# Finishing the first up tiles from SBUF and moving adaLN loads out of the w_o stage

## The chip, the core and the metric

The kernel runs on one NeuronCore of a Trainium2 chip. A core has five engines with an instruction stream each: TensorE (PE, with its weight loads shown apart as PEld) multiplies matrices into PSUM, VectorE (DVE) and ScalarE (ACT) do elementwise work, GpSimd (POOL) and SyncE (SP) are used here mostly to issue DMAs. An engine works through its stream in order and waits at an instruction until its operands are there. Work passes between engines through SBUF tiles and PSUM banks.

The metric is device time in microseconds for one execution of the whole program, as a median of several runs. A profile is one execution, recorded by the hardware.

## What is computed

One layer of a decoder trunk, for 512 tokens of width 2048, all in float32: a token-mixing part (stick-breaking attention, sparse attention with an index, two gates, an output projection `w_o`) and a gated MLP with a causal convolution of width 3. Both are modulated by a conditioning vector c (adaLN). Cut to what matters here:

```python
c_act = jax.nn.silu(c)
mod = c_act @ w_ada[layer] + b_ada[layer]
sh1, sc1, gt1, sh2, sc2, gt2 = jnp.split(mod[:, None, :], N_MOD, axis=-1)
h = rmsnorm(x, g_mix[layer]) * (1 + sc1) + sh1
x = x + (1 + gt1) * mixer(h, positions, w_in[layer], w_a[layer], w_b[layer], w_o[layer])
h = rmsnorm(x, g_ffn[layer]) * (1 + sc2) + sh2
x = x + (1 + gt2) * conv_ffn(h, w_up[layer], conv_w[layer], conv_b[layer], w_down[layer])
...
def conv_ffn(h, w_up, conv_w, conv_b, w_down):
    u = h @ w_up
    up = jnp.pad(u, ((0, 0), (CONV_WIDTH - 1, 0), (0, 0)))
    u = conv_b + sum(conv_w[i] * up[:, i:i + S] for i in range(CONV_WIDTH))
    a, b = jnp.split(u, 2, axis=-1)
    return (jax.nn.silu(a) * b) @ w_down
```

## The kernel before

**Arithmetic.** Every float32 operand is split into a high part and a rest (wh and wl for weights, lines 168 and 170; pairs of F tiles for activations, lines 197 and 199), and a product is three matmuls (lines 178 to 180). A weight chunk is loaded into one of eight buffers with the tag raw (128x1024, 512 KB), split by ScalarE (wh) and VectorE (wl) into one of three rooms, and then multiplied.

**Units.** Most projections run in `unit` (line 242), which computes two output tiles with seven half-width products of eight pairs each, 168 matmuls of 128x256, in place of eight products. A unit loads four weight quarters into raw, a fifth raw tile s takes their sums and differences (lines 268, 272, 306, 310), and the results are put together from three PSUM banks (lines 276, 308, 309, 312, 314). Units take their banks from acc and att in turn. `between` is called at two places of a unit with the last instructions there, so that other work can be queued behind them.

**Stages, in order.** Values and index queries; 31 units over `w_x` (u = 1 to 31, line 748); the second values projection, in whose sixteen steps the index scores are computed (line 877); eight stick-breaking heads; eight sparse heads (line 1057), with the projection by `w_a` between them; sixteen tiles by `w_b`, merged with the gates (lines 1092 and 1093); eight units over `w_o` (line 1177), the last of which carries the second norm along; the first six tiles of the up projection, done in the plain way (`plain`, line 1226) while the operands of the units are being made; 41 units over `w_up` (line 1357), each followed by `finish`; the down projection.

**adaLN.** mod is made on VectorE: `w_ada` is stored transposed, in tiles of 128 rows and two halves of 1024. A half is loaded into raw and multiplied by the broadcast c in one operation with a running sum (line 711, 1.22 us). 96 halves of tiles 32 to 79 are spread over the stages: `ada_load(n)` loads the next n and `some_ada(n)` takes n products, loading first if nothing is loaded. From the 49th half on, a second broadcast, cb[1], holds one of the eight raw buffers. Seven halves go through a tile of their own (soft, line 735). Tiles 32 to 47 are needed at the end of the sparse heads, 48 to 79 before the last w_o unit. In the kernel before, the w_x units take one each, five stick heads three each, the sparse heads 26 in all, w_b six, and the eleven that remain fall to the w_o units, where `between` calls `some_ada()` and `ada_load()` twice in a unit.

**The plain up tiles.** The first NU = 3 column tiles of each half of w_up are computed plainly in six PSUM banks. They are evacuated into six F tiles, saved to DRAM (ud, line 1295) and brought back one by one in the later up units by `finish_first`, a generator of which one step runs ahead of each unit from j = 9 on; it loads a tile (SP, line 1337), convolves it (ScalarE line 1330, VectorE line 1333), and saves the product (line 1353). `finish` does the same for the units' own tiles, from the F tiles that they return: `conv` (lines 1210 to 1212) into a tile w, of which there are two, a Silu (line 1217), a product (line 1219) and a save to yd by POOL.

**Slots.** F tiles (512 columns) come from a pool of 62. In the up stage 56 hold the operand forms of the units.

**Order.** The building framework orders each engine's instructions, allocates the tiles and sets the waits, by the order of the program and its own estimate of when an operand is ready. An instruction can be put ahead of the place where it stands in the program; `behind(ins)` holds what is traced inside it behind ins on ins's engine.

## Time and profile before

| | us |
|---|---|
| median of 3 runs | 2738.51 (2733.37 to 2740.41) |
| the profiled execution | 2737.63 |
| its span | 2735.7 |
| TensorE busy in the span | 2677.8 |
| VectorE busy | 2406.6 |
| ScalarE busy | 1448.4 |
| w_x units, first to last | 228 to 827 |
| index scores and second values | 827 to 901 |
| sparse heads | about 1010 to 1138 |
| w_b | 1139 to 1226 |
| w_o | 1226 to 1402 |
| plain up tiles | 1402 to 1475 |
| up units | from 1475 |

A row of the page's groups or of the timeline names a line of the kernel, an engine, an operation, the tiles out<-in with buffer numbers left out, their shapes and a count, then busy time and the mean of one in ns, and in the end how long the engine stood idle before it and what ended that. A row of the list of waits names who waited, at which line, for whom, with the total, the number of times and the longest. A row of the table by stretches has a stretch of time, its length, the busy time and the count of instructions of PE, PEld, DVE, ACT and POOL, the granted TensorE clock, the share of time in which the DMA engines were busy, and their GB/s. Matmuls are pipelined and their ends are modelled, so a matmul's duration is longer than the distance to the next; distances between starts are used for TensorE.

### The profile page before, as it was taken

To read this page: it belongs to the slowest core of one execution; us is meant where nothing else is said; L and a number is where in the kernel's file an instruction comes from. 1 tells how busy PE (TensorE), PEld (TensorE's weight loads), DVE (VectorE), ACT (ScalarE), POOL (GpSimd) and SP (SyncE) were. 2 spreads that over 40 slices of the span, in tenths; PEclk is the share of its full clock that TensorE was granted. 3 is DMA by queue.
4 is the path that set the end of the run, shared out by engine and by line. 5 is a ranking of instruction groups with operands and counts; after the bars stand their busy time and mean duration, and the time that the engine had idled before them with its cause. 6 is when DMAs were issued, how large, how long until landed. Compare 5 with 4: busy or idle time off the path is not lost.

```text
span 2735.7 us, 47661 instructions
## 1 busy us (share of the span) xinstructions
PE 2677.8 (98%) x18700; PEld 2453.8 (90%) x18700; DVE 2406.6 (88%) x3402; ACT 1448.4 (53%) x2037; POOL 315.8 (12%) x514
## 2 busy tenths in 40 slices
PE   8999999999999999999999999999999999999998
PEld 6789999999997778889999999999999998887876
DVE  8888989999987899798878999999999997888887
ACT  4444455554446665434466555555555455546443
POOL 0000010100012211112220000000000000003011
PEclk9999999999999999999999999999999999999999
DMA  9883556666676648766864666666666436468785
GB/s 351 326 301 123 174 199 196 192 212 220 205 227 203 199 140 285 237 206 216 243 215 136 189 175 189 173 181 175 171 177 181 132 125 223 154 179 236 207 228 166
DMA packets 167853, 551.65 MB, mean 202 GB/s; under 512 B 21750, under 2 KB 22390, under 8 KB 167628
## 3 DMA queue, kind: packets, MB, share of 16 engines
q1 hardware_dynamic: 119820, 408.49, 46.4%
q0 software_dynamic: 47216, 139.73, 18.7%
q8 instruction: 147, 2.41, 0.3%
q14 instruction: 78, 0.64, 0.1%
q10 hardware_dynamic: 592, 0.39, 0.1%
HBM read 453.97 MB, written 91.14 MB: 199 GB/s over the span
## 4 chain that ended last, share of the span: by engine, by line
PE 83%; DVE 8%; DMA 4%; issue 3%; ACT 2%; SPq 0%; POOL 0%; ACTq 0%; DVEq 0%; POOLq 0%
PE att L180 13%; PE att L179 13%; PE att L178 13%; PE acc L179 12%; PE acc L180 12%; PE acc L178 12%; DVE wl L170 2%; PE acc L928 1%; DMA F<-ud 1%; ACT wh L168 1%; DMA raw<-in_w_down 1%; PE outs L179 1%; PE outs L178 1%; PE outs L180 1%; PE acc L896 1%
## 5 line engine op out<-in xcount | busy, mean ns | idle before, releaser
L168 ACT ACTIVATE wh<-raw 128x1024 fp32r<-128x1024 f32 (+1 forms) x790 | 828.8, 1055 | 945.7 <-DVE raw L272 174.9
L170 DVE TENSOR_TENSOR wl<-raw,wh 128x1024 fp32r<-128x1024 f32 (+1 forms) x790 | 953.4, 1214 | 125.3 <-ACT wh L168 117.7
L178 PE MATMUL acc<-F,wh 128*128 128x256 f32 (+1 forms) x2448 | 702.3, 287 | 9.0 <-DVE sp L308 4.3
L178 PE MATMUL att<-F,wh 128*128 128x256 f32 (+1 forms) x2448 | 704.3, 288 | 6.2 <-DVE sp L308 5.2
L180 PE MATMUL acc<-F,wl 128*128 128x256 f32 (+1 forms) x2448 | 701.5, 287 | 8.1 <-DVE wl L170 8.1
L180 PE MATMUL att<-F,wl 128*128 128x256 f32 (+1 forms) x2448 | 702.3, 287 | 4.3 <-DVE wl L170 4.3
L179 PE MATMUL att<-F,wh 128*128 128x256 f32 (+1 forms) x2448 | 701.6, 287 | 0.2 <-DVE F L199 0.2
L179 PE MATMUL acc<-F,wh 128*128 128x256 f32 (+1 forms) x2448 | 701.2, 287 | 0.1
L178 PEld LDWEIGHTS acc<-F,wh 128*128 128x128 f32 x2448 | 460.2, 188 | 21.8 <-issue 5.1
L178 PEld LDWEIGHTS att<-F,wh 128*128 128x128 f32 x2448 | 461.6, 189 | 17.4 <-issue 5.7
L180 PEld LDWEIGHTS acc<-F,wl 128*128 128x128 f32 x2448 | 460.4, 188 | 18.1 <-DVE wl L170 9.3
L180 PEld LDWEIGHTS att<-F,wl 128*128 128x128 f32 x2448 | 461.7, 189 | 13.2 <-DVE wl L170 5.0
L179 PEld LDWEIGHTS att<-F,wh 128*128 128x128 f32 x2448 | 461.7, 189 | 8.8 <-DVE F L199 0.7
L179 PEld LDWEIGHTS acc<-F,wh 128*128 128x128 f32 x2448 | 460.5, 188 | 10.1 <-DVE F L490 0.8
L178 PE MATMUL att<-wh,F 128*128 128x512 f32 x448 | 177.8, 398 | 0.2 <-ACT wh L168 0.2
L179 PE MATMUL att<-wl,F 128*128 128x512 f32 x448 | 175.3, 391 | 0.7 <-DVE wl L170 0.7
L180 PE MATMUL att<-wh,F 128*128 128x512 f32 x448 | 175.1, 391 | 0.0
L179 PE MATMUL acc<-wl,F 128*128 128x512 f32 x288 | 113.5, 394 | 4.3 <-DVE wl L170 4.3
L268 DVE TENSOR_TENSOR raw<-raw,raw 128x1024 f32<-128x1024 f32 x80 | 97.4, 1218 | 18.9 <-DMA raw<-in_w_o 14.1
L178 PE MATMUL acc<-wh,F 128*128 128x512 f32 x288 | 112.4, 393 | 0.1
L180 PE MATMUL acc<-wh,F 128*128 128x512 f32 x288 | 111.3, 391 | 0.0
L711 DVE SCALAR_TENSOR_TENSOR raw<-raw,raw 128x1024 f32<-128x1024 f32 x89 | 107.3, 1217 | 0.8 <-DMA raw<-in_w_ada 0.8
(370 smaller groups left out, 3719.9 us busy)
## 6 DMA issues: line engine op xcount, KB each, us to landing
raw<-in_w_up SPq DMA_DIRECT2D x164, 512.0 KB, 3.8
raw<-in_w_ada SPq DMA_DIRECT2D x152, 512.0 KB, 5.2
raw<-in_w_x SPq DMA_DIRECT2D x128, 512.0 KB, 4.3
raw<-in_w_down SPq DMA_DIRECT2D x104, 512.0 KB, 4.5
xd<-F POOLq DMA_DIRECT2D x64, 256.0 KB, 3.0
F<-xd POOLq DMA_DIRECT2D x64, 256.0 KB, 4.9
raw<-in_w_o SPq DMA_DIRECT2D x32, 512.0 KB, 5.5
soft<-in_w_gate SPq DMA_DIRECT2D x32, 512.0 KB, 3.9
```

The lines of the kernel that those rows point to most:

```text
L168: pins["wh"] = act(wh, raw, AF.Copy)
L170: pins["wl"] = tt(wl, raw, wh.bitcast(F32), ALU.subtract)
L178: mm(ps, ah, bh, start=first, stop=False, skip_group_check=not check)
L179: mm(ps, ah, bl, start=False, stop=False, skip_group_check=not check)
L180: return mm(ps, al, bh, start=False, stop=last, skip_group_check=not check)
L268: last_v = tt(s, a21, a22, ALU.add)
L711: stt(w, w, 1.0, cb[half], ALU.mult, ALU.mult, accum_out=macc[:, t, half : half + 1])
L896: mm(zk, k[:, q0 : q0 + P], q[:, q0:], start=kb != 3, stop=False, skip_group_check=True)
L928: mm(o, negtri if tri else negones, i, start=False, stop=True, skip_group_check=True)
```

## The change

Plain up tiles: they are evacuated into slots and stay there. The save to ud and `finish_first` are gone, and `finish` runs on each pair of them ahead of the first, second and third up unit.

adaLN halves: three more are loaded and taken in the w_x units 29 and 30, two in the steps of the index scores (loaded at steps 3 and 9, taken at 6 and 12), and three more in each of the last two sparse heads, together eleven. In w_o `between` loads only at its first call and takes only at its second.

```diff
@@ for u in range(1, 32)
         def between(i, *pins):
+            free = u in (29, 30)
             if not i:
+                ada_load(2 if free else 1)
+            elif u == 29:
                 ada_load()
             with behind(*pins):
                 next(work)
-                if i:
-                    some_ada()
+                if i or u == 30:
+                    some_ada(2 if free and i else 1)
@@ index scores
     for i in range(16):
+        if i in (3, 9):
+            ada_load()
         run(fill, 2)
         run(index)
+        if i in (6, 12):
+            some_ada()
     run(fill)
@@ sparse heads
         last = sparse_2(p, s)
         run(fill)
+        if hd > 5:
+            ada_load(3)
         before = hd, sparse_3(p), vb[hd // 4]
         with behind(last):
-            some_ada(2 if hd else 0)
+            some_ada((2 if hd else 0) + (3 if hd > 5 else 0))
         run(fill, 2)
@@ w_o
     def between(i, *pins):
         turn()
         with behind(*pins):
-            some_ada()
-        ada_load()
+            if i:
+                some_ada()
+        if not i:
+            ada_load()
@@ up
             form(f[p], x1[2 * p], x1[2 * p + 1])
-    ud = dram("ud", 2 * NU)
-    for i, ps in enumerate(ups):
-        save(ud[i], evac(ps))
+    ups = [evac(ps) for ps in ups]
...
-    def finish_first():
...
-        for j in range(NU):
-            u = bring(2 * j)
-            yield
-            yield
-            for a in half(2 * j, u):
-                yield
-            act(a, a, AF.Silu)
-            u = bring(2 * j + 1)
-            yield
-            yield
-            for b in half(2 * j + 1, u):
-                yield
-            tt(a, a, b, ALU.mult)
-            save(yd[j // 2][:, j % 2 * S : (j % 2 + 1) * S], a)
-            yield
-
-    gate, first_tiles = last_gate(), finish_first()
+    gate = last_gate()
     for j in range(NU, NJ):
-        if 2 * NU <= j < 2 * NU + 2:
+        if j < 2 * NU:
+            finish(j - NU, *ups[2 * (j - NU) : 2 * (j - NU) + 2])
+        elif j < 2 * NU + 2:
             x = t2k("T", 2)
             save(x, x1d[KT - 2 + j - 2 * NU])
             to_turn.append((KT - 2 + j - 2 * NU, x))
-        if j >= 3 * NU:
-            run(first_tiles)
         finish(j, *unit(A["w_up"][j - NU], f, beside_up))
```

## The prediction

> **What bounds the kernel now.** I read the page first: its span and the busy times.

> ```profile
> span 2735.7 us, 47661 instructions
> PE 2677.8 (98%) x18700; PEld 2453.8 (90%) x18700; DVE 2406.6 (88%) x3402; ACT 1448.4 (53%) x2037; POOL 315.8 (12%) x514
> ```

> TensorE sets the time, with VectorE close behind. A change that touches no matmul can only win what TensorE loses in waits, so I looked for those. I took the start of the first matmul of every seven-product unit from the timeline and asked for the busy times between these starts. First the up stage (columns: stretch, length, then busy time and count of PE, PEld, DVE, ACT, POOL, granted clock, DMA share, GB/s):

> ```profile
> 1475.02:1493.97 18.95, 18.95 (x169) 18.95 (x168) 13.23 (x15) 10.68 (x14) 2.18 (x4) 1.00 0.65 209
> 1493.97:1513.01 19.04, 19.04 (x170) 19.04 (x169) 17.85 (x22) 12.27 (x15) 1.08 (x2) 1.00 0.53 174
> 1513.01:1532.06 19.05, 19.05 (x171) 19.05 (x170) 17.85 (x22) 10.99 (x14) 1.43 (x2) 1.00 0.61 165
> 1532.06:1551.58 19.52, 19.52 (x175) 19.52 (x174) 17.86 (x22) 11.59 (x15) 2.15 (x3) 1.00 0.71 194
> ```

> An undisturbed unit takes 19.04 us, its 168 matmuls end to end. The fourth has four transposes more (19.52). Of the later units eight are longer; they are the ones in which the plain up tiles come back from DRAM. Four of them, and the sum of all eight:

> ```profile
> ...
> 1764.55:1788.10 23.55, 21.17 (x170) 20.78 (x169) 19.21 (x24) 12.20 (x16) 1.42 (x2) 0.93 0.62 162
> 1845.22:1869.29 24.07, 21.26 (x171) 20.86 (x169) 19.69 (x25) 11.68 (x15) 1.98 (x3) 0.93 0.61 160
> 1945.45:1968.28 22.83, 20.98 (x170) 20.79 (x169) 19.21 (x24) 12.21 (x16) 1.42 (x2) 0.93 0.63 168
> 2025.40:2047.35 21.95, 19.62 (x171) 19.22 (x169) 19.07 (x25) 11.68 (x15) 1.98 (x3) 1.00 0.61 156
> ...
> sum 171.89, PE 160.40 PEld 158.24 DVE 151.44 ACT 93.77 POOL 13.04; mean PE 20.05 PEld 19.78 DVE 18.93 ACT 11.72 POOL 1.63
> ```

> Eight undisturbed units would be 8 x 19.04 = 152.32 us, so **19.6 us** are lost here. Next the stage that multiplies by w_o: its first five units, their sum, and the two that follow:

> ```profile
> 1226.17:1249.89 23.72, 20.07 (x170) 19.49 (x168) 23.12 (x34) 10.52 (x15) 1.07 (x2) 1.00 0.44 147
> 1249.89:1272.45 22.56, 20.25 (x178) 20.08 (x177) 18.36 (x24) 10.41 (x15) 4.55 (x7) 1.00 0.73 236
> ...
> 1293.84:1318.13 24.29, 21.44 (x178) 21.27 (x177) 19.48 (x24) 10.95 (x15) 6.46 (x10) 0.95 0.75 226
> ...
> sum 112.77, PE 102.75 PEld 101.51 DVE 96.58 ACT 51.92 POOL 22.04; mean PE 20.55 PEld 20.30 DVE 19.32 ACT 10.38 POOL 4.41
> ```

> ```profile
> 1338.94:1358.94 20.00, 20.00 (x178) 20.00 (x177) 17.48 (x20) 11.02 (x15) 6.36 (x10) 1.00 0.83 251
> 1358.94:1378.94 20.00, 20.00 (x178) 20.00 (x177) 16.39 (x19) 10.39 (x14) 5.45 (x9) 1.00 0.68 191
> ```

> With eight transposes a unit takes 20.00 us; the first unit has none. Undisturbed, the five would be 19.04 + 4 x 20.00 = 99.04 us, so **13.7 us** are lost. The remarkable thing is where the losses stop. The group of adaLN products of this stage is

> ```profile
> L711 DVE SCALAR_TENSOR_TENSOR raw<-raw,raw x11: 1215/1219/1226, 1216.6 to 1334.4; 128x1024 f32<-128x1024 f32 x11
> ```

> The last of the eleven starts at 1334.4, and from 1338.94 on each unit takes its exact 20.00.

> Then the list of waits, for the causes (total, times, longest):

> ```profile
> ACT T L1330 <- DMA F<-ud: 25.8, 6, 5.3
> ...
> DVE raw L268 <- DMA raw<-in_w_o: 14.1, 5, 4.6
> ```

> and the timeline at one stall of each kind:

> ```profile
> 1768.58 0.82 ACT L1330 ACTIVATE T<-F,cw 128x512 f32<-128x512 f32 x1 [4.90 <-DMA F<-ud]
> ```

> ```profile
> 1310.14 1.23 DVE L268 TENSOR_TENSOR raw<-raw,raw 128x1024 f32<-128x1024 f32 x1 [4.64 <-DMA raw<-in_w_o]
> ...
> 1312.42 1.22 DVE L711 SCALAR_TENSOR_TENSOR raw<-raw,raw 128x1024 f32<-128x1024 f32 x1
> ...
> 1313.56 0.42 DVE L308 TENSOR_TENSOR sp<-att,ta 128x256 f32<-128x256 f32 x1
> ```

> In the up stage ScalarE sits at L1330 for a tile that has only just been asked for; queued behind it is the wh split (L168) on which TensorE depends. In w_o VectorE sits at L268 for a weight quarter, because the adaLN halves hold raw buffers (cb[1], two halves and the unit's five tiles are all eight); then it does an adaLN product of 1.22 us, and only then L308, which frees the accumulator that TensorE waits for.

> Some stalls cost twice. The stretches before and after two of them:

> ```profile
> 1312.16:1315.57 3.41, 1.44 (x12) 1.47 (x13) 3.38 (x7) 0.38 (x1) 0.00 (x0) 1.00 0.57 142
> 1315.57:1318.99 3.42, 3.42 (x19) 3.42 (x18) 3.35 (x5) 0.63 (x1) 1.83 (x3) 0.50 0.70 242
> 1769.55:1772.96 3.41, 1.10 (x8) 0.70 (x6) 1.88 (x3) 3.41 (x6) 0.00 (x0) 1.00 0.78 274
> 1772.96:1776.37 3.41, 3.35 (x15) 3.35 (x16) 3.41 (x5) 1.04 (x2) 0.56 (x1) 0.50 0.03 12
> ```

> After 3.41 us with TensorE busy for 1.1 to 1.4 of them the granted clock is 0.50 for the next 3.41 us, which costs half of that, 1.7 us. The three up units with clock 0.93 have one such stretch each, w_o has one. These four are inside the 19.6 and 13.7.

> **Part one: plain up tiles from their slots.** Removed: six saves to ud on POOL's queue, six loads on SP's, and the 27 steps of finish_first. With them goes every wait at L1330, since the operand is now in SBUF. What is late next in those eight units? Nothing that shows: their neighbours, with the same loads, gate steps and finish, run at 19.04. So the whole 19.6 goes.

> Added: finish of one plain tile in each of the first three units. VectorE's share is two L1211, two L1212 and one L1219:

> ```profile
> L1211 DVE SCALAR_TENSOR_TENSOR w<-F,cw,w x82: 742/746/753, 1493.6 to 2283.5; 128x511 f32<-128x511 f32 x82
> ```

> At 0.746 us for each of the four (L1212 is one element shorter) and about 0.69 for the 512-wide product, that is 3.7 us per tile. The first unit has room: 13.2 + 3.7 = 16.9 of 18.95. The second and third do not: 17.85 + 3.7 = 21.5 in 19.04, 2.5 us over each; the two units after them have 1.7 us of room each. ScalarE has room everywhere (12.3 + 2.2 of 19). No row shows a unit of this form with VectorE over its time. Below: nothing, if the order lets a tile slip forward into the first unit and back into the fourth. Above: 2 x 2.5 of stall and a half-clock stretch in each, 5.0 + 3.4 = 8.4. The wl splits of the unit queue behind these operations. The nearest row is the first w_o unit, 23.1 of VectorE in 23.7 with no half clock, which loses about what VectorE is over; of 5.0 I take **2.0**, since 2.1 and 1.7 us of room lie before and after.

> Slots: 62, of which the forms hold 56 (each of the eight pairs six for T1 to T4 and B21, B22, every two pairs two for B11), and one x1 tile still waits to be transposed (its copy, L1116, runs in the first up unit, row below); with six plain tiles that is 63, so the last evacuation must wait for the first tile's convolution. Its bank is needed one unit later, and that convolution takes a few microseconds. I cost it at nothing; the slower rival is what happens if that cover is gone.

> **Part two: the adaLN halves.** w_o's eleven go: three to w_x units 29 and 30, two to the index scores, six to the last two sparse heads. Counted by the loops, none is left for w_o. Its units two to five should go to 20.00. In the first unit one product (L711) is gone from ahead of the merge (L1092), but that merge still has to follow the last w_b matmul, so I leave 1.2 us of its 4.7. Gain 13.7 - 1.2 = **12.5**.

> What the halves cost where they land, from these rows (w_x units 29 to 31; index scores; a stick stretch with the highest traffic; sparse heads 5, 6, 7):

> ```profile
> 768.64:788.56 19.92, 19.92 (x173) 19.44 (x172) 16.21 (x19) 9.78 (x13) 4.71 (x6) 1.00 0.76 194
> 788.56:807.60 19.04, 19.04 (x171) 19.04 (x170) 17.68 (x22) 9.40 (x12) 0.56 (x1) 1.00 0.82 262
> ...
> 850.00:875.00 25.00, 24.80 (x110) 18.05 (x109) 23.17 (x37) 22.19 (x43) 5.35 (x10) 1.00 0.50 154
> ...
> 948.00:969.00 21.00, 19.85 (x92) 14.67 (x91) 19.47 (x48) 10.22 (x16) 9.59 (x18) 1.00 0.99 357
> 1088.30:1104.70 16.40, 16.40 (x88) 13.61 (x87) 15.06 (x34) 8.79 (x18) 3.17 (x7) 1.00 0.84 288
> 1104.70:1121.20 16.50, 16.50 (x89) 13.71 (x88) 11.64 (x28) 6.15 (x14) 2.15 (x4) 1.00 0.75 258
> 1121.20:1137.60 16.40, 16.40 (x98) 14.32 (x97) 11.59 (x27) 6.15 (x14) 1.61 (x3) 1.00 0.80 256
> ```

> - w_x: unit 29 takes one product more (16.2 + 1.2 of 19.92), unit 30 two (17.7 + 2.4 = 20.1 of 19.04), and three halves besides five unit tiles fill the eight raw buffers, the very state of w_o. SP's loads for the next unit queue behind them. Between nothing and two units at the 2.56 us of the second w_o unit, 5.1; I take **1.5**, as the pressure lasts for part of two units and 29 has 3.7 us of room.
> - Index scores: VectorE is at 23.2 of 25. Two products are 2.4 us; between 0 and 2.4 I take **1.2**.
> - Sparse heads 6 and 7: VectorE 11.6 + 3 x 1.22 = 15.3, what head 5 carries with TensorE full. Traffic: 3 x 0.524 MB in 16.4 us is 96 GB/s more, 354 in all, as in the 948 to 969 stretch, where TensorE lacked 1.15 of 21 us. Over two heads that is 1.8 at most; SP's w_a and w_b loads queue behind these. I take **1.0**.

> **The sum.** The profiled execution took 2737.6 us (span 2735.7 and 1.9 around it); the median is 2738.5, 0.9 more. 2737.6 - 19.6 + 2.0 - 12.5 + 1.5 + 1.2 + 1.0 = 2711.2, and 0.9 on top is **2712**. All costs at their upper ends give 2712 + 6.4 + 3.6 + 1.2 + 0.8 = 2724; none, with all 33.3 won, gives 2705.

> **Rivals.**
> - *The adaLN part nets nothing.* The full raw buffers, not the stage, make the stalls, and they move with the halves. For: units 29 and 30 get the same count. Against: room on VectorE in three of the four places. Price 12.5 less the 3.7 already counted: 2721.
> - *VectorE becomes the bound in the first up units*, with half clocks: 2.0 becomes 8.4, 2718.
> - *The half-clock stretches stay.* Price 4 x 1.7, 2719. Against: both rows above follow an almost idle stretch. [...]
> - *Adding both first rivals at their ends*: 2724 + 8.8 = 2733, no change that can be told.
> - *Slower: slots starve the first up unit.* If its first output gets a slot only after the third plain tile is finished, TensorE stands for three finishes in a row. The first finish of before, from its first ScalarE operation to its product, the copy of the waiting tile, and the view of the tile yd for its saves:

> ```profile
> 1481.21 0.59 ACT L1116 ACTIVATE F<-outs 128x512 f32<-128x512 f32 x1
> ...
> 1492.31 0.80 ACT L1210 ACTIVATE w<-F,cw 128x512 f32<-128x512 f32 x1
> ```

> ```profile
> 1500.15 0.69 DVE L1219 TENSOR_TENSOR w<-w,w 128x512 f32<-128x512 f32 x1
> ```

> ```profile
> DMA to landing us min/median/max: 2.3/2.3/9.8
> ```

>   One takes 8.5 us, and 2.3 more until its save gives a w buffer back: 3 x 10.8 = 32.4. With 0.6 + 2.3 for the waiting tile and 1.7 of half clock that is 37.0, and 2712 - 2 + 37 = 2747. It decides if fewer than two slots are free four products into that unit. Against: the second tile's convolution needs nothing but those slots' own contents and could run as early as the first's.

> **How the numbers follow.** Forecast 0.62, adaLN nets nothing 0.13, VectorE-bound up units 0.12, half clocks stay 0.04, both first at their ends 0.05, slot starvation 0.04. A measurement of this kernel tells about 0.3%, 8.2 us, from no change. Faster by more (under 2730.3): the first four, 0.91; within: 0.05; slower: 0.04. The range goes from 2703 (2705 and the scatter of the runs) to 2725; it holds all but the last two cases.

> **What would show it.** Right: no F<-ud in the list of waits, up units at 19.04 throughout, w_o units at 20.00, no clock of 0.93 in either stage. Wrong: up units two and three over 21.5 or the first one with a wait on a slot; w_x units 30 and 31 over 20.5 with L268 waiting for in_w_x; heads 6 and 7 over 17.5 with a wait for in_w_a or in_w_b. Most harmful to the forecast would be an order of instructions that changes away from these places, where the rows say nothing.

## The result and the profile after

| | us | runs |
|---|---|---|
| before, beside the changed kernel | 2739.19 median | 4 |
| after | 2715.30 median (2711.95 to 2718.44) | 4 |
| ratio over all runs, not of the two medians | 0.9917, 95% interval 0.9898 to 0.9935 | |
| the profiled execution after | 2715.49, span 2713.6 | |

The forecast of 2712 lay 3 us under the median. The page's first lines after:

```profile
span 2713.6 us, 47640 instructions
PE 2673.0 (99%) x18700; PEld 2449.8 (90%) x18700; DVE 2407.1 (89%) x3402; ACT 1447.5 (53%) x2037; POOL 311.8 (11%) x508
```

The busy time of VectorE and ScalarE is what it was. Of the 22.1 us between the two spans 17.3 are idle time of TensorE and 4.8 are busy time (2677.8 to 2673.0) at the same 18700 matmuls; a 128x256 matmul in a stretch of granted clock 0.50 counts as busy for 0.42 us (384.17 in the trace before), at 1.00 for 0.28 (385.01 after). I took the start of the first matmul of each stage and unit in both traces and compared the distances:

| stretch | forecast | measured, us |
|---|---|---|
| eight late up units | -19.6 | -19.6 |
| second to fourth up unit | +2.0 | +5.4 |
| first five w_o units | -12.5 | -11.6 |
| w_x units 29 to 31 | +1.5 | +4.8 |
| end of w_x to the first w_b tile | +2.2 | +1.4 |
| everything else | 0 | -2.5 |

The two large gains came as forecast. Two costs came out at about three times their size (2.7 and 3.2 times). In the last row, w_x unit 8 (-1.5) and the norm between w_o and the up stage (+1.5) differ by stretches of half clock (last section); the down projection (-1.3) and the time after the last matmul (-1.1) were not traced further.

The eight late units, in the table by stretches of the kernel after (two of them, and the sum of all eight):

```profile
1590.01:1609.05 19.04, 19.04 (x170) 19.04 (x169) 17.84 (x22) 10.99 (x14) 1.42 (x2) 1.00 0.65 179
...
2027.93:2046.97 19.04, 19.04 (x170) 19.04 (x169) 17.84 (x22) 10.99 (x14) 1.42 (x2) 1.00 0.67 183
sum 152.32, PE 152.32 PEld 152.32 DVE 142.70 ACT 87.87 POOL 11.34; mean PE 19.04 PEld 19.04 DVE 17.84 ACT 10.98 POOL 1.42
```

152.32 is exactly 8 x 19.04, against 171.89 before. The first two w_o units and the sum of five:

```profile
1230.72:1251.86 21.14, 19.97 (x170) 19.40 (x169) 20.62 (x30) 10.74 (x15) 1.84 (x4) 1.00 0.37 126
1251.86:1271.85 19.99, 19.99 (x178) 19.99 (x177) 16.38 (x19) 10.37 (x14) 4.63 (x8) 1.00 0.67 198
...
sum 101.13, PE 99.96 PEld 99.39 DVE 86.16 ACT 52.22 POOL 22.86; mean PE 19.99 PEld 19.88 DVE 17.23 ACT 10.44 POOL 4.57
```

From the second unit on, VectorE has 16.4 us of work in 20.0; before it had 18.4 on the mean of these four, (96.58 - 23.12) / 4 by the prediction's sum. The first unit keeps 2.1 us over 19.04.

Now the costs. First the up units two to four:

```profile
1488.40:1509.82 21.42, 20.15 (x174) 19.67 (x173) 19.47 (x26) 12.41 (x17) 1.61 (x3) 1.00 0.54 185
1509.82:1531.46 21.64, 20.19 (x170) 19.45 (x169) 20.72 (x27) 13.63 (x19) 2.72 (x4) 1.00 0.39 105
1531.46:1551.44 19.98, 19.60 (x170) 19.24 (x169) 19.09 (x23) 11.70 (x15) 1.43 (x2) 1.00 0.74 227
```

The three take 63.04 us; before it was 57.61 (19.04 + 19.05 + 19.52, the second, third and fourth rows of the prediction's up stage). The four transposes of the fourth unit have moved to the second. That is 1.9, 2.6 and 0.9 us over. TensorE has no half clock here, and VectorE is not busy throughout: 19.47 of 21.42 in the second. One of the other causes stands in ScalarE's timeline in the second unit:

```profile
1498.84 0.82 ACT L1221 ACTIVATE w<-F,cw 128x512 f32<-128x512 f32 x1 [1.72 <-DMA yd<-w]
```

L1221 is the first operation of `conv` (L1210 before). It needs one of the two w tiles, and both are still being saved or finished. The wh splits of the unit (L168) stand behind it in ScalarE's stream, so they are held back too.

Then w_x unit 29, which took 19.92 us before:

```profile
767.03:791.46 24.43, 21.68 (x173) 21.03 (x172) 18.25 (x23) 9.88 (x13) 4.63 (x6) 0.93 0.71 189
791.46:810.50 19.04, 19.04 (x171) 19.04 (x170) 17.84 (x24) 9.40 (x12) 0.91 (x3) 1.00 0.86 290
```

VectorE was not short of time here: 18.25 busy of 24.43. Its timeline shows what it stood for, and the stretches show what TensorE made of it:

```profile
785.43 1.23 DVE L268 TENSOR_TENSOR raw<-raw,raw 128x1024 f32<-128x1024 f32 x1 [4.18 <-DMA raw<-in_w_x]
786.58 0.42 DVE L308 TENSOR_TENSOR sp<-att,ta 128x256 f32<-128x256 f32 x1
```

```profile
783.50:786.92 3.42, 0.89 (x8) 0.69 (x7) 1.49 (x3) 0.14 (x1) 0.00 (x0) 1.00 1.07 293
786.92:790.33 3.41, 3.19 (x15) 3.22 (x16) 3.41 (x7) 1.21 (x2) 0.00 (x0) 0.50 0.26 39
```

This is the picture of w_o before, moved: L268, which already works for unit 30, waits 4.18 us for a weight quarter, L308 of unit 29 behind it frees the accumulator, TensorE idles 2.5 us and then runs 3.41 us at half clock (1.7 lost). The quarters of unit 30 are loaded during unit 29, and they were issued late. SP's rows of that time, after and then before:

```profile
759.08 10.77 SPq L702 DMA_DIRECT2D raw<-in_w_ada  x3
773.53 5.80 SPq L154 DMA_DIRECT2D raw<-in_w_x  x4
```

```profile
762.96 13.93 SPq L154 DMA_DIRECT2D raw<-in_w_x  x4
```

A row spans the issues that it holds and the waits among them. With three adaLN halves in front of them in SP's stream, which take 10.77 us to get their buffers, the first of the four quarters was issued 10.6 us later than before, though the unit itself began 1.6 us sooner (767.03 against 768.64). L268 needs the second and the third quarter. The third was issued at 777.86, 10.8 us into the unit, where before it was 6.5 (775.14). It then took 7.5 us to land in place of 4.4; that the four now follow one another in 5.8 us and not in 13.9 is my guess at the cause, which no run shows alone. So about 4.3 us of the lateness is the issue and 3.1 the landing.

### The profile page after: what moved, and what is told of

Same layout as the page of the kernel before. It is cut to its first block, busy times and chain, and to the rows that moved or that the text cites. A ratio compares the mean times of both kernels' runs of the same rounds, so it can differ in the third digit from the quotient of the medians.

```text
span 2713.6 us, 47640 instructions
## 1 busy us (share of the span) xinstructions
PE 2673.0 (99%) x18700; PEld 2449.8 (90%) x18700; DVE 2407.1 (89%) x3402; ACT 1447.5 (53%) x2037; POOL 311.8 (11%) x508
## 4 chain that ended last, share of the span: by engine, by line
PE 82%; issue 7%; DVE 5%; DMA 3%; ACT 2%; POOL 1%; SPq 0%; ACTq 0%; POOLq 0%; DVEq 0%
PE att L180 12%; PE att L178 12%; PE att L179 12%; PE acc L179 12%; PE acc L178 12%; PE acc L180 12%; DVE wl L170 1%; PE outs L179 1%; PE outs L178 1%; PE outs L180 1%; DMA raw<-in_w_down 1%; PE outs L1042 1%; PE acc L935 1%; PE acc L1011 1%; PE acc L837 0%
## 5 line engine op out<-in xcount | busy, mean ns | idle before, releaser
L168 ACT ACTIVATE wh<-raw 128x1024 fp32r<-128x1024 f32 (+1 forms) x790 | 829.1, 1055 | 938.6 <-DVE raw L272 184.8
L178 PEld LDWEIGHTS acc<-F,wh 128*128 128x128 f32 x2448 | 458.6, 187 | 20.1 <-issue 5.1
L711 DVE SCALAR_TENSOR_TENSOR raw<-raw,raw 128x1024 f32<-128x1024 f32 x89 | 106.8, 1216 | 1.4 <-DMA raw<-in_w_ada 1.4
L268 DVE TENSOR_TENSOR raw<-raw,raw 128x1024 f32<-128x1024 f32 x80 | 97.2, 1215 | 8.6 <-DMA rope<-raw 4.2
```

The costliest lines, as they stand in the source:

```text
L168: pins["wh"] = act(wh, raw, AF.Copy)
L178: mm(ps, ah, bh, start=first, stop=False, skip_group_check=not check)
L268: last_v = tt(s, a21, a22, ALU.add)
L711: stt(w, w, 1.0, cb[half], ALU.mult, ALU.mult, accum_out=macc[:, t, half : half + 1])
```

## The experiments

Four questions were open: whether the two parts are independent, whether raw buffers make the stall of unit 29, what makes the 5.4 us in the first up units, and whether both costs can be avoided. A time without a range is a single run.

**E1: the part of the plain tiles alone.** adaLN as before (the loops over w_x, the index scores, the sparse heads and w_o restored), the up stage as after.

> The plain up tiles finished from slots, the adaLN halves left as before. Theory (the two parts add up): the eight late up units go to 19.04 us (-19.6), units two to four of the up stage lose 2.4 + 2.6 + 0.5 = 5.4 us as in the changed kernel, the w_o units stay at 23.7, 22.6, 21.4, 24.3 and 20.8 us; time 14.1 us below before, about 2725 us. Rival (the parts act on each other): the loss in the first up units comes from the shifted adaLN work; then it is under 2 us here and the time is below 2721 us.

2722.81 us (2720.56 to 2725.17) against 2735.65 before in the same session; ratio 0.9952, interval 0.9934 to 0.9970: 12.8 us won. The units two and three of the up stage, and the first w_o unit:

```profile
1494.84:1516.28 21.44, 20.15 (x175) 19.68 (x174) 19.47 (x26) 12.42 (x17) 1.62 (x3) 1.00 0.56 183
1516.28:1537.93 21.65, 20.23 (x171) 19.50 (x169) 20.72 (x27) 13.63 (x19) 2.72 (x4) 1.00 0.42 106
```

```profile
1226.02:1249.64 23.62, 20.02 (x169) 19.43 (x168) 23.19 (x34) 10.43 (x15) 1.07 (x2) 1.00 0.47 147
```

The up stage repeats that of after to 0.02 us, and w_o is as disturbed as before. 19.6 less 5.4 is 14.2, 1.4 more than was won. In the profile the norm between w_o and the up stage takes 1.5 us longer than before (two stretches of half clock in place of one, last section), which the edit does not touch.

**E2: the adaLN part alone.** The plain tiles go through ud as before.

> The adaLN halves moved, the plain up tiles left as before. Theory (the parts add up): w_o units two to five at 20.00 us and the first at about 21.1 (-11.6), w_x unit 29 longer by 4.5 us or, without a half-clock stretch behind its gap, by about 2.9, index stage 1.4 longer, the eight late up units still 19.6 us over; time 4 to 6 us below before, 2733 to 2735 us. Rival (the adaLN part nets nothing, the whole win is the up part): within 1 us of before.

2728.04 us (2725.15 to 2732.02), ratio 0.9974, interval 0.9963 to 0.9985: 7.6 us won, more than the 4 to 6 expected; the excess was not traced. Unit 29 and the second w_o unit:

```profile
769.81:794.55 24.74, 21.78 (x172) 21.14 (x171) 18.36 (x23) 9.89 (x13) 4.71 (x6) 0.93 0.69 186
```

```profile
1253.74:1273.74 20.00, 20.00 (x179) 20.00 (x177) 16.39 (x19) 10.37 (x14) 4.65 (x8) 1.00 0.67 197
```

Both the gain and its price belong to this part. 12.8 + 7.6 = 20.4 us. The whole change won 23.9 by the medians above and 19.2 when it was run again (E8), and the product of the two ratios, 0.9926, lies inside its interval of 0.9898 to 0.9935. So the parts add up, within the scatter. The rival that adaLN nets nothing has fallen, as the interval excludes 1, though what it names did happen in one unit.

**E3: the plain tiles finished in T tiles.** If the wait for a w tile makes the 5.4 us, other tiles take it away; if VectorE's time does, they change little.

```diff
-    def conv(u, j):
-        t = t2k("w", 2)
+    def conv(u, j, tag="w"):
+        t = t2k(tag, 2)
...
-            finish(j - NU, *ups[2 * (j - NU) : 2 * (j - NU) + 2])
+            finish(j - NU, *ups[2 * (j - NU) : 2 * (j - NU) + 2], "T")
```

> The changed kernel with the plain tiles' convolutions in the two T tiles in place of the two w tiles, so that no finish waits for a w tile that a save to yd still holds. Theory (VectorE has more work than time in the second and third up unit, 2 x 2.5 us): up units two to four stay together about 5.4 us over (5 to 6). Rival (ScalarE's waits of 1.7 and 0.4 us for yd hold back the wh splits): the waits are gone and the three units are together under 3.5 us over.

2712.29 us. The units two and three:

```profile
1486.50:1508.25 21.75, 19.64 (x171) 19.24 (x169) 20.86 (x26) 12.08 (x16) 2.16 (x4) 1.00 0.53 169
1508.25:1528.23 19.98, 19.35 (x171) 19.15 (x169) 18.32 (x23) 11.21 (x14) 1.99 (x3) 1.00 0.68 196
```

```profile
1489.42 0.82 ACT L1221 ACTIVATE T<-F,cw 128x512 f32<-128x512 f32 x1 [2.96 <-DMA yd<-T]
```

2.7 + 0.9 = 3.6 us over: between the two expectations, and the wait had not gone. The second tile's finish slipped forward into the first unit, and the third's then waited 2.96 us for the T tile being saved. Inconclusive; E9 repeats it with the order held.

**E4: a ninth raw buffer under E2's kernel,** paid for with two of the 62 slots.

```diff
-SLOTS = 62
+SLOTS = 60
...
-        raw = t2k("raw", 8, w=w)
+        raw = t2k("raw", 9, w=w)
```

> The adaLN move alone with nine raw buffers in place of eight (and 60 slots in place of 62 to make room). Only w_x unit 29 is looked at. Theory (the third adaLN load of unit 29 and the loads for unit 30 stand in one queue and wait for raw buffers): with one buffer more the third half is loaded at once, the w_x loads start up to 10 us earlier, L268 waits at most 2 us for in_w_x, and unit 29 takes at most 21.5 us. Rivals (VectorE's two more products, or the traffic of the two more loads, make the gap): unit 29 still has a gap of 2.5 to 3 us and takes 22.7 to 24.5 us.

Unit 29, SP's loads in it for unit 30, and L268 in it:

```profile
766.22:786.85 20.63, 20.20 (x172) 19.55 (x171) 16.76 (x22) 9.26 (x12) 4.12 (x5) 1.00 0.74 191
```

```profile
768.66 8.72 SPq L154 DMA_DIRECT2D raw<-in_w_x  x4
```

```profile
781.18 1.23 DVE L268 TENSOR_TENSOR raw<-raw,raw 128x1024 f32<-128x1024 f32 x1 [1.86 <-issue]
```

20.63 us in place of 24.74. The loads start 2.4 us into the unit (768.66 - 766.22) and not 6.5 as in the kernel after (773.53 - 767.03) and in E2. L268 still waits 1.86 us. The row puts that down to no DMA, but in the trace the third quarter lands at 781.10, 0.08 us before L268 starts, so it is the same wait, 4.39 us in E2, made shorter. There is no half clock. So the full raw buffers make most of this stall. The whole kernel took 2733.45 us in its one run, over E2's 2728.04: the ninth buffer or the two slots cost elsewhere more than is won here, which was not traced further.

**E5: the same three more halves in w_x, but two in each of the units 28 to 30,** and each pair taken at the second call.

```diff
-            free = u in (29, 30)
+            n = 2 if u in (28, 29, 30) else 1
             if not i:
-                ada_load(2 if free else 1)
-            elif u == 29:
-                ada_load()
+                ada_load(n)
             with behind(*pins):
                 next(work)
-                if i or u == 30:
-                    some_ada(2 if free and i else 1)
+                if i:
+                    some_ada(n)
```

> The changed kernel with the three extra adaLN halves of the w_x stage taken one each in units 28, 29 and 30: two loads at the first call, two products at the second, so that a unit holds seven raw buffers at its fullest and not eight. VectorE's work and the traffic over the three units are the same. Theory (raw buffers run out): units 28 to 30 are together at most 1 us over their 19.92, 19.92 and 19.04, and unit 29 loses its 4.5 us. Rival (the products themselves are too many for these units): the gaps are spread, together 2 to 4.5 us.

2707.86 us. The units 28 to 30:

```profile
745.58:766.48 20.90, 20.20 (x172) 19.55 (x171) 16.76 (x20) 9.89 (x13) 4.16 (x6) 1.00 0.81 218
766.48:786.78 20.30, 20.18 (x172) 19.53 (x171) 17.04 (x21) 9.78 (x13) 4.68 (x7) 1.00 0.75 191
786.78:805.82 19.04, 19.04 (x170) 19.04 (x169) 18.28 (x25) 9.29 (x12) 1.38 (x3) 1.00 0.89 304
```

They took 19.92, 19.92 and 19.04 before, so the three halves cost 1.4 us here and not 4.5: somewhat more than the 1 us expected. The half clock is gone, and of the stall of 4.18 us at L268 1.56 us are left. VectorE's products and the traffic over the three units are the same, so it was not their amount that made the 4.5.

**E6: the second and third plain tile finished one operation at a time,** in a generator of which one step runs behind the second call's instructions of each later unit, without the way through DRAM, and in T tiles. The two x1 tiles that pass through T are brought later (at j = 15 and 16), and their transposes with them.

```diff
+            if i:
+                run(first_tiles)
...
+        for j in range(1, NU):
+            ab = []
+            for c in (2 * j, 2 * j + 1):
+                u, t = ups[c], t2k("T", 2)
+                act(t, u, AF.Identity, scale=cw[:, c, 2:3], bias=cw[:, c, 3:4])
+                stt(t[:, 1:], u[:, : S - 1], cw[:, c, 1:2], t[:, 1:], ALU.mult, ALU.add)
+                yield
+                stt(t[:, 2:], u[:, : S - 2], cw[:, c, 0:1], t[:, 2:], ALU.mult, ALU.add)
...
+        if j == NU:
+            finish(0, *ups[:2])
```

> The changed kernel with the first plain tile finished ahead of the first up unit and the two others in steps of one VectorE operation behind each of the next ten units, from their slots, in T tiles. Theory (the first units were over because two whole finishes stood in each): up units two to four go from 5.4 us over to at most 1 us over, and no later unit is over 19.6 us but the two with transposes (19.52). Rival (slots: the tiles held longer leave none for the units' outputs): units two to ten wait for a slot and are together over 3 us longer than 19.04 each.

2711.91 us. The units two and three:

```profile
1486.76:1505.80 19.04, 19.04 (x170) 19.04 (x169) 18.33 (x23) 11.39 (x15) 1.08 (x2) 1.00 0.56 178
1505.80:1524.84 19.04, 19.04 (x170) 19.04 (x169) 18.41 (x23) 11.57 (x15) 1.43 (x2) 1.00 0.60 166
```

All up units take 19.04 but those with transposes (19.52 to 19.54) and four late ones with the gate's matmuls (20.23, in all kernels): the 5.4 us are gone, though plain tiles now hold slots for longer. So it was the way the finishes were packed, not their work, and slots are not short.

**E7 and E8: E5 and E6 together, beside the changed kernel itself on the same chip.**

> Both of the last two edits together. If both theories hold, 5.4 + 2.9 to 4.5 us less than the changed kernel on the same chip, that is 8 to 10 us, 0.30 to 0.37%; if only the up theory holds 4 to 6 us; if neither, within 2 us.

> The changed kernel itself once more, beside the last one on the same chip: 0.8 to 1.0% below before. In its profile the adaLN and up losses stand where they stood (w_x unit 29 about 22.8 to 24.5 us, up units two and three 21.4 and 21.6 us); half-clock stretches with no long gap of their own may lie elsewhere.

| | us | ratio to before (2734.45, 11 runs) | interval |
|---|---|---|---|
| E7, both spread | 2704.51 (2704.26 to 2706.46, 6 runs) | 0.9885 | 0.9866 to 0.9904 |
| E8, the change again | 2715.22 (2713.16 to 2716.18, 6 runs) | 0.9922 | 0.9904 to 0.9939 |

The ranges are 6.7 us apart, the medians 10.7, 0.4%. E7 beats both kernels, by a little more than the 8 to 10 us expected. Its units 28 to 30 take 20.00, 20.94 and 19.04, 1.1 over in place of 4.5, and its up units 19.04: 3.4 + 5.4 = 8.8 of the 10.7; the rest was not traced, and the two profiles also differ by 2.4 us ahead of unit 28, where the programs are the same. E8 comes out nearly as expected: 0.78% below before, unit 29 at 24.42 us, up units two and three at 21.44 and 21.66.

**E9: as E3, with each of the two finishes held behind the unit's second call,** and the first tile in w.

```diff
-            finish(j - NU, *ups[2 * (j - NU) : 2 * (j - NU) + 2])
+            with behind(*unit_pins):
+                finish(j - NU, *ups[2 * (j - NU) : 2 * (j - NU) + 2], "T" if j > NU else "w")
```

> Like the run with T tiles, which let the second plain tile slip forward into the first up unit and still had a wait for a T tile. Here the first plain tile uses w tiles, the second and third use the T tiles and are held behind the second call of the first and second up unit, so that two finishes meet at each of these boundaries with no tile that a save holds. Theory (VectorE's work at one place is the limit): with no wait of ScalarE for yd, the first four up units are still together 4 to 6 us over 19.54, 19.04, 19.04 and 19.52. Rival (the wait for the save of yd was the cause): under 2.5 us over.

2711.13 us. The units two to four:

```profile
1485.12:1505.69 20.57, 19.92 (x171) 19.36 (x170) 20.57 (x27) 12.91 (x17) 1.62 (x3) 1.00 0.51 175
1505.69:1526.52 20.83, 20.05 (x175) 19.76 (x173) 19.64 (x24) 11.91 (x15) 3.81 (x6) 1.00 0.65 191
1526.52:1545.56 19.04, 19.04 (x171) 19.04 (x169) 17.84 (x22) 10.99 (x14) 1.43 (x2) 1.00 0.73 194
```

No operation of ScalarE waits for a save to yd any more. The sum is 60.44 against 57.61, and the first unit keeps its 19.54: 2.8 us over, again between the two expectations and nearer to the lower. In the second unit VectorE is busy for 20.57 of 20.57, so that part is its own time. Of the 5.4 us roughly half remains without the wait and roughly half goes with it; the order of the instructions, the transposes among them, changed too, so this split is an approximation and not settled. The changed kernel's own trace points the same way: its chain of work that ended last runs in the second unit through the save of 1496.50 to 1498.81 and ScalarE behind it, and in the third, from 1512.9 to 1523, through VectorE's operations.

## Why the prediction was right, and where not

- **Late up units, right.** 19.6 forecast, 19.6 measured, and E1 gives it to this part alone. What stood next in line really was nothing: 17.84 of VectorE in 19.04. (The prediction's list of longer units leaves out four at 20.23 us, which carry the gate's matmuls and are the same in both kernels.)
- **w_o, right.** 12.5 forecast, 11.6 measured. The step that failed by 0.9 is what the first unit keeps: 1.2 by the forecast, 2.1 by the trace.
- **First up units, mechanism right, size off: 2.0 became 5.4.** The step was that the neighbours' room takes up what VectorE is over. The operations stayed where `finish` stands, VectorE ran over in the second and third unit, and the fourth took only 0.9 of it, as delay. A second cause was missing from this term: the w tiles. The prediction has the 2.3 us of the save, but only in the slower rival; E9 suggests that it is about half. The third unit's 21.64 is just over the 21.5 that the prediction named as a sign of being wrong. The upper bound of 8.4 held, and no half clock came: no stretch of 3.41 us there had TensorE idle for more than 1.9. (The prediction's first row starts 0.6 us behind that unit's first matmul, at 1474.43; the room there comes out at 2.0 instead of 2.1 us, which changes nothing.)
- **w_x, mechanism named, size off: 1.5 became 4.8.** The prediction had the full raw buffers and SP's queue in this term, and then let VectorE's 3.7 us of room in unit 29 lower the price. That room does not help against this stall, because VectorE was the engine that waited (4.18 us at L268). The nearest row was the worst w_o unit with a half clock (24.29 for 20.00), not the second one with 2.56. It came in unit 29, not in 30 and 31 where the prediction told the reader to look. E4 and E5 show the cause from two sides.
- **Index scores and sparse heads, 2.2 forecast, 1.4 measured.** From the start of the sparse heads to the first w_b tile the time is the same to 0.1 us, so six more products and loads cost nothing there. Over the whole stretch from w_x to w_b the kernels of eight raw buffers with adaLN unmoved took 311.8 to 312.4 us and those with it moved 312.2 to 313.9, so the 1.4 is hardly more than the scatter.
- **Slots, right.** No wait on a slot showed.
- **The rivals.** That the half-clock stretches stay fell: in both stages they went with the gaps, though what the prediction calls almost idle was 1.10 and 1.44 us of work in 3.41. That adaLN nets nothing fell by E2. VectorE as the bound was part of the truth, at 5.4 and not at 8.4.

The errors of the terms were +3.4, +3.3, +0.9 and -0.8, together 6.8; the table's last row hid 2.5 of it, and the median of after lies under its profile by 0.2 where that of before lay 0.9 above. So the number was nearer than its terms, by luck.

## What to carry to other kernels

Price a moved load by the buffer that it holds and by the queue in which it stands ahead of others, asking when the load that is waited for gets issued, and not by the busy time of the engine that uses it: room on that engine was worth nothing in unit 29 (18.25 us busy of 24.43) while it waited 4.18 us for its own operand. Side work that ran whole in one unit competed with that unit for its engine and its scratch tiles (5.4 us over three units); the same work, one operation per unit, held behind a fixed instruction, cost nothing here (E6, units of 19.04). And when a stall vanishes with a full pool of buffers, look for the next place where that pool will be full.

## What the runs showed of the hardware

```profile
380.32:383.73 3.41, 1.21 (x10) 1.24 (x11) 2.92 (x4) 1.06 (x1) 1.07 (x2) 1.00 0.95 371
383.73:387.15 3.42, 3.42 (x18) 3.42 (x17) 3.39 (x6) 0.00 (x0) 0.54 (x1) 0.50 0.63 170
```

```profile
380.73:384.15 3.42, 1.62 (x14) 1.65 (x15) 3.33 (x5) 1.06 (x1) 1.07 (x2) 1.00 0.99 376
384.15:387.56 3.41, 3.41 (x33) 3.41 (x32) 3.38 (x5) 0.00 (x0) 0.54 (x1) 1.00 0.57 172
```

The granted clock is the column before the last two. The same gap falls a little earlier or later against the grid: with 1.21 us of work in its stretch the next one runs at 0.50, with 1.62 it does not, and the unit takes 24.07 us or 22.53. Since a matmul's end is modelled, I also worked out idle time from the distances between matmul starts, with each form of matmul taken at its median distance at full clock, for every stretch at full clock in the traces of before and after, the end of each program left out. 26 stretches had between 1.2 and 1.95 us idle, and none was followed by 0.50, nor were two with 2.04 and 2.05. All nine with more were: six from 2.06 to 2.29, and three of 2.57, 2.69 and 2.75. The two stretches above come out at 2.29 and 1.90.

So in these two traces some 2 us idle of 3.41, about 60%, was followed by the half clock, with 0.89 and 1.21 us of work still in the stretch in two of the rows shown; how sharp the border near 2.05 is, such a sum does not tell. A gap of over 2 us thus risked up to 1.7 us more here, half of a stretch of 3.41 (1.5 between the two times of unit 8), and which kernel paid was a matter of phase: the norm between w_o and the up stage has one such stretch of 3.4 us before and two after, w_x unit 8 has one before and none after, and neither was edited. The changed kernel run again (E8) shows it without any change of program: no such stretch at that norm, where its other profile has two, and one in unit 8 (23.53 us), where the other has none.
